# A log-sum-exp kernel on one core: VectorE's jump behind the last sum, checks joined, one exponential for four folded rows, the small logarithm one piece later

## The chip, the core and the metric

One core of a Trainium2 chip runs the kernel. The metric is device time in microseconds of one execution; a median of several runs is given, and one more execution is recorded by the hardware profiler. Shorter is better.

## The reference

The input is 32 x 512 rows of 1024 fp32 numbers, 64 MiB in all; the output is one number for each row.

```python
def reference(x):
    max_x = np.max(x, axis=-1, keepdims=True)
    return (max_x.squeeze(-1) + np.log(np.sum(np.exp(x - max_x), axis=-1))).astype(np.float32)
```

## The kernel before

The kernel takes the exponential without subtracting the maximum, adds up, and takes the logarithm. Beside that it checks that every sum lies between 1e-15 and 1e15 (and that the first elements of one row aren't too large); a flag is read back, and only where a check fails a slow path inside an `If` computes everything anew with the maximum. On ordinary data that path is skipped.

The 16384 rows are 128 partitions times 128 rows. The first 112 rows of each partition (`W`) come in nine loads (`LOADS`) into a ring of 48 rows in the on-chip memory; all loads are issued by SyncE (SP), each as soon as the users of the buffer that it overwrites are done. The string beside each size in `LOADS` says how the load is summed. Each word is one exponential on ScalarE (ACT), in place:

- `R16`: VectorE (DVE) sums 16 whole rows with one reduction (L237).
- `F4`: GpSimd (POOL) first adds the second half of each of four rows to the first (L231), and VectorE later sums the half rows (L190, `reduce_folded`). A pending fold is summed at the next `F`, or after the next `R`.

The last 16 rows of each partition (`B`) come in nine late pieces (`late`), cut at sizes of their own and not at rows: 3760 elements from the first rows, 3488 from the last four, then 2656, 2000, 1456, 1088 and 800 through the middle, then the last row's end (610 with two joining numbers) and the first row's head (530 with two). Each gets one exponential (L280, the last two L273 and L265). After each, VectorE sums the rows that have become complete, one instruction for a row, which adds the row's halves and accumulates (L199, `halves`); the profile shows a second, short instruction for each, the read of the accumulator. The first and last rows are each split over two pieces. The part of each that comes early is summed by itself (`parts`), and the logarithm of half of it is written twice into the ring beside the piece that comes late (`joined`, the small logarithm of L310, on 4 numbers), so that the exponential of that piece, which accumulates, adds it in.

When the second late piece is through, ScalarE takes the logarithms of the first 112 rows (L302), and VectorE checks these sums and the two parts (`check_early`, L159 and L164). The sums of the late rows are added up on TensorE (PE) in `count` (L177, `add_up`), so that a number that isn't finite shows there.

At the end ScalarE takes the logarithms of 15 late rows (L321) and of the first late row (L323), SyncE stores them (L325), VectorE checks the 15 sums (L330) and the head's elements (L340), PE adds the outcome to `count`, and VectorE turns it into the flag `fine` (L347). ScalarE and VectorE read it and branch over the slow path (L403). SyncE waits for that and for the stores, and resets the semaphores (L406, L408).

Waits are written by hand: `Counted.wait` lets an engine wait for another's count, and instructions of one engine run in program order. The line `nc.vector.addr_align(128, offset=0, max_nops=0)` (L284) puts the next VectorE instruction at a multiple of 128 instruction slots; the padding is jumped over. In the kernel before it stands ahead of the sum of the row that the 800-wide piece completes, which is VectorE's last row sum.

Of the kernel before, what the change touches and what calls it, by code (L numbers as in the profile page):

```python
# [12 lines left out]
LOW, HIGH = 1e-15, 1e15  # L13
# [3 lines left out]
B = 16  # L17
# [4 lines left out]

LOADS = [
    (16, "R16"), (16, "R16"), (16, "R16"), (16, "F9 R7"), (13.5, "F6 R7"), (12.5, "R7 F6"),
    (9, "R5 F4"), (7, "F4 R3"), (6, "F2 F2 R2"),
]


# [28 lines left out]
def kernel(  # L57
# [5 lines left out]
    nc = tc.nc  # L63
# [4 lines left out]
    P = nc.NUM_PARTITIONS  # L68
    fp32 = mybir.dt.float32
    i32 = mybir.dt.int32  # L70
    AF = mybir.ActivationFunctionType
    AX = mybir.AxisListType
    ALU = mybir.AluOpType

    x_flat = x.flatten_outer_dims()
    n, d = x_flat.shape
    assert n % P == 0
    NC = n // P
    H = d // 2
    W = NC - B  # L80
# [6 lines left out]
    def source(e0, size):  # L87
# [1 line left out]
        return x_rest[:, e0 - W * d : e0 - W * d + size] if e0 >= W * d else x_rows[:, e0 : e0 + size]  # L89

    loads = [
        (int(size * d), [(op[0], 0 if op[0] == "Y" else int(op[1:] or 1)) for op in ops.split()])
        for size, ops in LOADS
    ]
    assert sum(size for size, _ in loads) == W * d
    assert sum(s for _, ops in loads for _, s in ops) == W
    start = MID * d - sum(PIECES)
    late = [(HEAD, start), (MID * d, B * d - BACK)]
    for size in PIECES:
# [1 line left out]
        start += size  # L101
    late += [(B * d - BACK, B * d), (0, HEAD)]
    assert start == MID * d and sum(e - s for s, e in late) == B * d

    def sbuf(name, cols, dtype=fp32, rows=P):
        return nc.alloc_sbuf_tensor(name, [rows, cols], dtype).ap()

    ring = sbuf("ring", RING * d)
    sums_all = sbuf("sumexp", 2 + NC)
    parts, sumexp = sums_all[:, 0:2], sums_all[:, 2 : 2 + NC]  # L110
    res = sbuf("res", NC)
    clamped = sbuf("clamped", NC)
    bad = sbuf("bad", 3)
# [11 lines left out]
    act = Counted(nc, nc.scalar, "act")  # L125
    dve = Counted(nc, nc.vector, "dve")
    pe = Counted(nc, nc.tensor, "pe")
    pool = Counted(nc, nc.gpsimd, "pool")
# [25 lines left out]
        ]  # L154

    def check_early():
        n = 2 + W
        dve.wait(dve, dve.n)
        dve.did(nc.vector.tensor_scalar(  # L159
            out=clamped[:, 0:n], in0=sums_all[:, 0:n],  # L160
            scalar1=LOW, scalar2=HIGH, op0=ALU.max, op1=ALU.min,
        ))
        dve.wait(dve, dve.n)
        dve.did(nc.vector.scalar_tensor_tensor(  # L164
            out=clamped[:, 0:n], in0=clamped[:, 0:n], scalar=0.0, in1=sums_all[:, 0:n],
            op0=ALU.bypass, op1=ALU.not_equal, accum_out=bad[:, 0:1],
        ))
        pe.wait(dve, dve.n)
        pe.did(nc.tensor.matmul(count, lhsT=bad[:, 0:1], rhs=far, start=True, stop=False))  # L169
# [3 lines left out]
    def add_up():  # L173
        while sums:
            c, who, at = sums.pop(0)
            pe.wait(who, at)
            pe.did(nc.tensor.matmul(  # L177
                count, lhsT=ones, rhs=sumexp[:, c : c + 1], start=False, stop=False
            ))

    folded = []
# [15 lines left out]
    def halves(v, c):  # L197
        n = v.shape[1] // 2
        return dve.did(nc.vector.scalar_tensor_tensor(  # L199
            out=v[:, 0:n], in0=v[:, 0:n], scalar=1.0, in1=v[:, n : 2 * n],  # L200
            op0=ALU.mult, op1=ALU.add, accum_out=c,
        ))

    c = 0
    p = 0
# [4 lines left out]
    for i, (size, ops) in enumerate(loads):  # L210
        if here + size > RING * d:
            assert here == p
            p = here = 0
        if any(q < here + size and q + t * d > here for _, t, q, _ in folded):
            reduce_folded()
        dma = load(i, here, done_before, size)
        if i < AHEAD:
            first_loads.extend(x.ins for x in dma)
        end = here + size
        done_before += size  # L220
        act.wait(landed[i], 16 * len(dma))
        for k, (how, s) in enumerate(ops):
            rows = ring[:, p : p + s * d].rearrange("p (c d) -> p c d", d=d)
            upto = end if k + 1 == len(ops) else p + s * d
            v = ring[:, here:upto]
            at = act.did(nc.scalar.activation(out=v, in_=v, func=AF.Exp))  # L226
            here = upto
            if how == "F":
                reduce_folded()
                pool.wait(act, at)  # L230
                at = pool.did(nc.gpsimd.tensor_tensor(  # L231
                    out=rows[:, :, 0:H], in0=rows[:, :, 0:H], in1=rows[:, :, H:d], op=ALU.add
                ))
                folded.append((c, s, p, at))
            else:
                dve.wait(act, at)
                at = dve.did(nc.vector.reduce_sum(out=sumexp[:, c : c + s], in_=rows, axis=AX.X))  # L237
                users.append((p, p + s * d, dve, at))
                early_sum = at
                reduce_folded()  # L240
            c += s
            p += s * d
        assert here == end
# [4 lines left out]
    def place(e0):  # L248
        return e0 - MID * d + p if e0 >= MID * d else gap + GAP + e0

    joins = bass.AP(
        tensor=ring.tensor, offset=ring[:, gap : gap + 1].offset,
        ap=[ring.ap[0], [GAP - 2, 2], [1, 2]],
    )
    summed = set()
    seen = []
    for k, (s, e) in enumerate(late):
        i = len(loads) + k
        at0, at1 = place(s), place(s) + e - s
        [dma] = load(i, at0, W * d + s, e - s)  # L260
        act.wait(landed[i], 16)
        if k >= len(late) - 2:
            act.wait(act, joined)
        if k == len(late) - 1:
            head_sum = act.did(nc.scalar.activation(  # L265
                out=last_exp[:, 0 : e - s + 2], in_=ring[:, at0 - 2 : at1], func=AF.Exp,
                accum_out=last_sum,
            ))
            break
        if k == len(late) - 2:  # L270
            assert at1 == gap
            v = ring[:, at0 : at1 + 2]
            back_sum = act.did(nc.scalar.activation(  # L273
                out=v, in_=v, func=AF.Exp, accum_out=sumexp[:, NC - 1 : NC]
            ))
            sums.append((NC - 1, act, back_sum))
            add_up()
            continue
        v = ring[:, at0:at1]
        at = act.did(nc.scalar.activation(out=v, in_=v, func=AF.Exp))  # L280
        if k == 0:
            reduce_folded()
        if k == len(late) - 3:
            nc.vector.addr_align(128, offset=0, max_nops=0)  # L284
        dve.wait(act, at)
        seen.append((s, e))
        for r in range(1, B - 1):
            left = r * d
            for s0, e0 in sorted(seen):
                if s0 <= left < e0:  # L290
                    left = e0
            if r not in summed and left >= (r + 1) * d:
                summed.add(r)
                row = ring[:, place(r * d) : place(r * d) + d]
                sums.append((W + r, dve, halves(row, sumexp[:, W + r : W + r + 1])))
        if k == 0:
            halves(ring[:, at0 : place(0) + d], parts[:, 1:2])
        if k == 1:
            halves(ring[:, place((B - 1) * d) : at1], parts[:, 0:1])
            both = dve.n  # L300
            act.wait(dve, early_sum)
            ln_early = act.did(nc.scalar.activation(  # L302
                out=res[:, 0:W], in_=sumexp[:, 0:W], func=AF.Ln
            ))
            check_early()
        if k >= 1:
            add_up()
        if k == 2:
            act.wait(dve, both)
            joined = act.did(nc.scalar.activation(  # L310
                out=joins, in_=parts[:, :, None].to_broadcast([P, 2, 2]), func=AF.Ln, scale=0.5
            ))
    assert len(summed) == B - 2

# [1 line left out]
    sp.wait(landed[-2], 16)  # L316
    nc.sync.dma_start(out=out_rows, in_=res[:, 0:W]).then_inc(sp.sem, 16)

    act.wait(dve, dve.n)
    act.wait(act, back_sum)  # L320
    act.did(nc.scalar.activation(out=res[:, W + 1 : NC], in_=sumexp[:, W + 1 : NC], func=AF.Ln))  # L321
    act.wait(act, head_sum)
    act.did(nc.scalar.activation(out=res[:, W : W + 1], in_=last_sum, func=AF.Ln))  # L323
    sp.wait(act, act.n)
    nc.sync.dma_start(out=out_rest, in_=res[:, W:NC]).then_inc(stored, 16)  # L325


    dve.wait(dve, dve.n)
    dve.wait(act, back_sum)
    dve.did(nc.vector.scalar_tensor_tensor(  # L330
        out=clamped[:, W + 1 : NC], in0=sumexp[:, W + 1 : NC], scalar=LOW,
        in1=sumexp[:, W + 1 : NC], op0=ALU.max, op1=ALU.not_equal, accum_out=bad[:, 1:2],
    ))
    pe.wait(dve, dve.n)
    pe.did(nc.tensor.matmul(count, lhsT=bad[:, 1:2], rhs=far, start=False, stop=False))
    pe.wait(dve, less_at)
# [4 lines left out]
        out=over, in0=ring[:, at0 : at0 + half], scalar=CEILING,  # L341
        in1=ring[:, at0 + half : at1], op0=ALU.max, op1=ALU.max, accum_out=bad[:, 2:3],
    ))
    pe.wait(dve, dve.n)
    at = pe.did(nc.tensor.matmul(count, lhsT=bad[:, 2:3], rhs=steep, start=False, stop=True))  # L345
# [12 lines left out]
    with nc.If(all_fine < 1):  # L358
# [3 lines left out]
        rows = 0  # L362
# [100 lines left out]
```

## Time and profile before

| | us |
|---|---|
| median of 3 runs | 161.93 (161.88 to 162.07) |
| profiled execution, its own time | 161.83 |
| its span, first to last instruction | 160.1 |
| ScalarE busy | 114.5 |
| VectorE busy | 114.2 |
| GpSimd busy | 37.3 |
| PE busy | 2.5 |

The DMA queue that loads the input moves 67.18 MB in all and has packets under way for 97.8% of 16 engines' span. Times in the profile are counted from the span's start; 1.7 of the profiled execution's own time lie outside the span. The first 116 us are the same kind of work in larger portions. The change touches what comes after the ninth load has landed, at about 138, so the views shown below are of that end.

### The profile page before, as it was taken

Reading aid. Unit: us, or ns where it says so; the run is one execution under the profiler, and the core shown is the slowest. Engines: PE = TensorE matmul, PEld = TensorE weight load, DVE = VectorE, ACT = ScalarE, POOL = GpSimd, SP = SyncE. Lnnn points to the kernel's source line nnn. Section 1 sums busy time; section 2 is a strip of 40 time slices with the busy share of each in tenths; the row PEclk is TensorE's granted clock in tenths of the full one; section 3 lists DMA queues with packets and bytes.
Section 4 is the critical chain, followed back from the end, with each engine's and each line's share of the span. In section 5 each row is a group of like instructions: output and inputs, shape, how many; then the busy total and the mean of one; then the engine's idle time right before and its main releaser. Section 6 shows DMA issues by size and latency. Waiting matters only on the chain.

```text
span 160.1 us, 250 instructions
## 1 busy us (share of the span) xinstructions
PE 2.5 (2%) x38; PEld 1.3 (1%) x38; DVE 114.2 (71%) x60; ACT 114.5 (71%) x32; POOL 37.3 (23%) x11
## 2 busy tenths in 40 slices
PE   0000000000000000000000000000000000000033
PEld 0000000000000000000000000000000000000011
DVE  0000000019999499994999859959999999999986
ACT  3000059980799709995099949992999989799996
POOL 0000000000000000000000993690004979891000
DMA  8995996996996996997999999999999999999993
GB/s 319 507 507 254 507 524 262 524 524 262 524 524 262 524 524 262 524 475 311 483 442 442 442 426 409 409 409 472 405 396 454 458 409 393 421 437 425 414 402 114
DMA packets 3025, 67.18 MB, mean 420 GB/s; under 512 B 592, under 2 KB 592, under 8 KB 1488
## 3 DMA queue, kind: packets, MB, share of 16 engines
q1 hardware_dynamic: 3024, 67.18, 97.8%
q14 instruction: 1, 0.01, 0.0%
HBM read 67.11 MB, written 0.07 MB: 419 GB/s over the span
## 4 chain that ended last, share of the span: by engine, by line
DMA 51%; ACT 27%; DVE 20%; issue 0%; PE 0%
DMA ring<-in_x_dram 51%; ACT ring L226 19%; DVE sumexp L237 16%; ACT ring L280 7%; DVE sumexp L190 2%; DVE ring L199 2%; DVE over L340 0%; PE count L345 0%; ACT res L302 0%; DVE clamped L330 0%; DVE fine L347 0%; ACT ring L310 0%
## 5 line engine op out<-in xcount | busy, mean ns | idle before, releaser
L226 ACT ACTIVATE ring<-ring 128x16384 f32<-128x16384 f32 (+9 forms) x16 | 98.0, 6169 | 42.3 <-DMA ring<-in_x_dram 42.3
L237 DVE TENSOR_REDUCE sumexp<-ring 128x16 f32<-128x16384 f32 (+4 forms) x9 | 85.6, 9514 | 42.0 <-ACT ring L226 42.0
L231 POOL TENSOR_TENSOR ring<-ring 128x3072 f32<-128x3072 f32 (+3 forms) x7 | 37.1, 5314 | 107.1 <-ACT ring L226 107.1
L190 DVE TENSOR_REDUCE sumexp<-ring 128x6 f32<-128x3072 f32 (+3 forms) x7 | 18.4, 2659 | 0.0
L280 ACT ACTIVATE ring<-ring 128x3760 f32<-128x3760 f32 (+6 forms) x7 | 13.7, 2006 | 0.0
L199 DVE SCALAR_TENSOR_TENSOR ring<-ring 128x512 f32<-128x512 f32 (+2 forms) x16 | 9.6, 652 | 0.4 <-ACT ring L280 0.3
L135 ACT ACT_TABLE_LOAD x1 | 1.3, 1283 | 1.9 <-PEq L66 1.9
L169 PE MATMUL count<-far,bad 128*1 128x1 f32 x2 | 0.2, 164 | 152.6 <-DVE clamped L164 152.6
L177 PE MATMUL count<-sumexp,ones 128*1 128x1 f32 x30 | 2.0, 163 | 3.6 <-DVE ring L199 3.5
L136 DVE MEMSET ones<- 128x1 f32 x1 | 0.1, 59 | 2.0 <-PEq L66 2.0
L169 PEld LDWEIGHTS count<-far,bad 128*1 128x1 f32 x2 | 0.1, 82 | 152.6 <-DVE clamped L164 152.6
L199 DVE DVE_READ_ACCUMULATOR ring<-ring 128x1 f32 x16 | 1.4, 85 | 0.0
L177 PEld LDWEIGHTS count<-sumexp,ones 128*1 128x1 f32 x30 | 1.1, 81 | 4.5 <-DVE ring L199 4.5
L273 ACT ACTIVATE ring<-ring 128x610 f32<-128x610 f32 x1 | 0.7, 696 | 0.0
L265 ACT ACTIVATE last_exp<-ring 128x530 f32<-128x530 f32 x1 | 0.6, 595 | 0.0
L340 DVE SCALAR_TENSOR_TENSOR over<-ring 128x264 f32<-128x264 f32 x1 | 0.4, 428 | 0.0
L347 DVE TENSOR_SCALAR fine<-count 1x1 int32<-1x1 f32 x1 | 0.1, 146 | 0.3 <-PE count L345 0.3
L164 DVE SCALAR_TENSOR_TENSOR clamped<-clamped,sumexp 128x114 f32<-128x114 f32 x1 | 0.3, 279 | 0.0
L302 ACT ACTIVATE res<-sumexp 128x112 f32<-128x112 f32 x1 | 0.3, 278 | 0.0
L159 DVE TENSOR_SCALAR clamped<-sumexp 128x114 f32<-128x114 f32 x1 | 0.2, 221 | 0.0
L321 ACT ACTIVATE res<-sumexp 128x15 f32<-128x15 f32 x1 | 0.2, 203 | 0.0
L330 DVE SCALAR_TENSOR_TENSOR clamped<-sumexp 128x15 f32<-128x15 f32 x1 | 0.2, 174 | 0.0
(20 smaller groups left out, 2.3 us busy)
## 6 DMA issues: line engine op xcount, KB each, us to landing
ring<-in_x_dram SPq DMA_DIRECT2D x1, 7936.0 KB, 21.2
ring<-in_x_dram SPq DMA_DIRECT2D x1, 6912.0 KB, 23.9
ring<-in_x_dram SPq DMA_DIRECT2D x1, 6400.0 KB, 19.7
ring<-in_x_dram SPq DMA_DIRECT2D x1, 4608.0 KB, 15.9
ring<-in_x_dram SPq DMA_DIRECT2D x1, 3584.0 KB, 24.0
ring<-in_x_dram SPq DMA_DIRECT2D x1, 3072.0 KB, 19.1
ring<-in_x_dram SPq DMA_DIRECT2D x1, 1880.0 KB, 16.0
ring<-in_x_dram SPq DMA_DIRECT2D x1, 1744.0 KB, 19.8
```

What stands on the lines that cost most here:

```text
L135: nc.scalar.preload_act_table_set("natural_log_exp_and_others")
L169: pe.did(nc.tensor.matmul(count, lhsT=bad[:, 0:1], rhs=far, start=True, stop=False))
L177: pe.did(nc.tensor.matmul(count, lhsT=ones, rhs=sumexp[:, c : c + 1], start=False, stop=False))
L190: at = dve.did(nc.vector.reduce_sum(out=sumexp[:, c0 : c0 + s0], in_=halves, axis=AX.X))
L199: return dve.did(nc.vector.scalar_tensor_tensor(out=v[:, 0:n], in0=v[:, 0:n], scalar=1.0, in1=v[:, n : 2 * n], op0=ALU.mult, op1=ALU.add, ...
L226: at = act.did(nc.scalar.activation(out=v, in_=v, func=AF.Exp))
L231: at = pool.did(nc.gpsimd.tensor_tensor(out=rows[:, :, 0:H], in0=rows[:, :, 0:H], in1=rows[:, :, H:d], op=ALU.add))
L237: at = dve.did(nc.vector.reduce_sum(out=sumexp[:, c : c + s], in_=rows, axis=AX.X))
L265: head_sum = act.did(nc.scalar.activation(out=last_exp[:, 0 : e - s + 2], in_=ring[:, at0 - 2 : at1], func=AF.Exp, accum_out=last_sum,))
L273: back_sum = act.did(nc.scalar.activation(out=v, in_=v, func=AF.Exp, accum_out=sumexp[:, NC - 1 : NC]))
L280: at = act.did(nc.scalar.activation(out=v, in_=v, func=AF.Exp))
L340: dve.did(nc.vector.scalar_tensor_tensor(out=over, in0=ring[:, at0 : at0 + half], scalar=CEILING, in1=ring[:, at0 + half : at1], op0=ALU.m ...
```

## The change

Four edits:

- The ninth load, `F2 F2 R2`, becomes `F2+2 R2`: one exponential over four rows in place of two over two rows each. GpSimd still folds them as two pairs, and VectorE still sums two pairs. Since both folds are pending when the two straight rows come, VectorE sums the straight rows first and both pairs after them; before, the first pair came ahead of the straight rows.
- The jump moves from ahead of VectorE's last row sum to behind it, ahead of the final check.
- The checks are joined: the first row's early part now lies in that row's column of the sums, so that one early check covers the first 112 rows, both parts and the three late rows summed with the first late piece. The final check covers 12 sums instead of 15, and the three rows are no longer added up on PE. The final check is written ahead of the last logarithms, and ScalarE's wait ahead of the logarithms of the 15 rows is now for this check instead of the last row sum.
- The small logarithm (`joined`) is taken after the exponential of the 2000-wide piece instead of the 2656-wide one.

```diff
-    (9, "R5 F4"), (7, "F4 R3"), (6, "F2 F2 R2"),
+    (9, "R5 F4"), (7, "F4 R3"), (6, "F2+2 R2"),
...
+    LATE = W + late[0][1] // d
...
-    sums_all = sbuf("sumexp", 2 + NC)
-    parts, sumexp = sums_all[:, 0:2], sums_all[:, 2 : 2 + NC]
+    sums_all = sbuf("sumexp", 1 + NC)
+    sumexp = sums_all[:, 1 : 1 + NC]
+    part_15, part_0 = sums_all[:, 0:1], sumexp[:, W : W + 1]
...
     def check_early():
-        n = 2 + W
+        n = 1 + LATE
...
             c, who, at = sums.pop(0)
+            if c < LATE:
+                continue
...
-                at = pool.did(nc.gpsimd.tensor_tensor(
-                    out=rows[:, :, 0:H], in0=rows[:, :, 0:H], in1=rows[:, :, H:d], op=ALU.add
-                ))
-                folded.append((c, s, p, at))
+                r = 0
+                for m in groups:
+                    lo = rows[:, r : r + m, 0:H]
+                    at = pool.did(nc.gpsimd.tensor_tensor(
+                        out=lo, in0=lo, in1=rows[:, r : r + m, H:d], op=ALU.add
+                    ))
+                    folded.append((c + r, m, p + r * d, at))
+                    r += m
...
-        if k == len(late) - 3:
-            nc.vector.addr_align(128, offset=0, max_nops=0)
         dve.wait(act, at)
...
-        if k == 2:
+        if k == 3:
             act.wait(dve, both)
             joined = act.did(nc.scalar.activation(
-                out=joins, in_=parts[:, :, None].to_broadcast([P, 2, 2]), func=AF.Ln, scale=0.5
+                out=joins, in_=parts, func=AF.Ln, scale=0.5
             ))
...
+    nc.vector.addr_align(128, offset=0, max_nops=0)
+    dve.wait(dve, dve.n)
+    dve.wait(act, back_sum)
+    dve.did(nc.vector.scalar_tensor_tensor(
+        out=clamped[:, LATE:NC], in0=sumexp[:, LATE:NC], scalar=LOW,
+        in1=sumexp[:, LATE:NC], op0=ALU.max, op1=ALU.not_equal, accum_out=bad[:, 1:2],
+    ))
     act.wait(dve, dve.n)
-    act.wait(act, back_sum)
     act.did(nc.scalar.activation(out=res[:, W + 1 : NC], in_=sumexp[:, W + 1 : NC], func=AF.Ln))
     act.wait(act, head_sum)
     act.did(nc.scalar.activation(out=res[:, W : W + 1], in_=last_sum, func=AF.Ln))
     sp.wait(act, act.n)
     nc.sync.dma_start(out=out_rest, in_=res[:, W:NC]).then_inc(stored, 16)
-
-
-    dve.wait(dve, dve.n)
-    dve.wait(act, back_sum)
-    dve.did(nc.vector.scalar_tensor_tensor(
-        out=clamped[:, W + 1 : NC], in0=sumexp[:, W + 1 : NC], scalar=LOW,
-        in1=sumexp[:, W + 1 : NC], op0=ALU.max, op1=ALU.not_equal, accum_out=bad[:, 1:2],
-    ))
```

More of the change, by code (lines that the diff above doesn't have):

```diff
@@ L91 @@
     loads = [
-        (int(size * d), [(op[0], 0 if op[0] == "Y" else int(op[1:] or 1)) for op in ops.split()])
+        (int(size * d), [(op[0], [int(s) for s in op[1:].split("+")]) for op in ops.split()])
         for size, ops in LOADS
@@ L95 @@
     assert sum(size for size, _ in loads) == W * d
-    assert sum(s for _, ops in loads for _, s in ops) == W
+    assert sum(sum(s) for _, ops in loads for _, s in ops) == W
     start = MID * d - sum(PIECES)
@@ L108 @@
     ring = sbuf("ring", RING * d)
-    sums_all = sbuf("sumexp", 2 + NC)
-    parts, sumexp = sums_all[:, 0:2], sums_all[:, 2 : 2 + NC]
+    sums_all = sbuf("sumexp", 1 + NC)
+    sumexp = sums_all[:, 1 : 1 + NC]
+    part_15, part_0 = sums_all[:, 0:1], sumexp[:, W : W + 1]
+    parts = bass.AP(
+        tensor=sums_all.tensor, offset=sums_all.offset,
+        ap=[sums_all.ap[0], [1 + W, 2], [0, 2]],
+    )
     res = sbuf("res", NC)
@@ L221 @@
         act.wait(landed[i], 16 * len(dma))
-        for k, (how, s) in enumerate(ops):
+        for k, (how, groups) in enumerate(ops):
+            s = sum(groups)
             rows = ring[:, p : p + s * d].rearrange("p (c d) -> p c d", d=d)
@@ L296 @@
         if k == 0:
-            halves(ring[:, at0 : place(0) + d], parts[:, 1:2])
+            halves(ring[:, at0 : place(0) + d], part_0)
         if k == 1:
-            halves(ring[:, place((B - 1) * d) : at1], parts[:, 0:1])
+            halves(ring[:, place((B - 1) * d) : at1], part_15)
             both = dve.n
```

## The prediction

> **What bounds the kernel now.** I read the chain of waits first, then the stages of the end, then the landings of single loads against the starts of the exponentials that consume them. The chain (start, length, what):
>
> ```profile
> 137.97 5.51 ACT ring L226 x3
> ...
> 155.44 1.10 DVE ring L199 x3
> ```
>
> From here the end looks like ScalarE's (ACT): from 137.97 the chain runs over the exponentials of the ninth load and then over those of the late pieces, and VectorE (DVE) comes in at 155.44. An edit that shortens ScalarE should then pay in full. The stages (busy time by engine, then granted clock, DMA share, GB/s) give a second candidate:
>
> ```profile
> core 0: us, PE busy (x) PEld busy (x) DVE busy (x) ACT busy (x) POOL busy (x), PEclk, DMA share, GB/s
> 137.90:143.40 5.50, 0.00 (x0) 0.00 (x0) 5.50 (x3) 5.43 (x4) 4.79 (x3) 1.00 1.01 432
> 149.60:154.00 4.40, 0.87 (x18) 0.56 (x18) 4.03 (x17) 4.40 (x6) 0.00 (x0) 1.00 1.00 411
> ```
>
> DMA, ScalarE and VectorE are all full, so no busy share decides. What decides is which of them is later at each piece. For three of the late pieces I take the issue (time, length) and the time to landing from the DMA view of the same instant, and then the exponentials:
>
> ```profile
> 127.70 0.46 SPq L150 DMA_DIRECT2D ring<-in_x_dram  x1
> ring<-in_x_dram SPq DMA_DIRECT2D x1, 1000.0 KB, 24.4
> 135.44 0.33 SPq L150 DMA_DIRECT2D ring<-in_x_dram  x1
> ring<-in_x_dram SPq DMA_DIRECT2D x1, 728.0 KB, 18.5
> 136.81 0.44 SPq L150 DMA_DIRECT2D ring<-in_x_dram  x1
> ring<-in_x_dram SPq DMA_DIRECT2D x1, 304.0 KB, 20.3
> ```
>
> ```profile
> 152.20 1.85 ACT L280 ACTIVATE ring<-ring 128x2000 f32<-128x2000 f32 x1
> 153.99 1.42 ACT L280 ACTIVATE ring<-ring 128x1456 f32<-128x1456 f32 x1
> 155.34 1.11 ACT L280 ACTIVATE ring<-ring 128x1088 f32<-128x1088 f32 x1
> 156.35 0.85 ACT L280 ACTIVATE ring<-ring 128x800 f32<-128x800 f32 x1
> 157.11 0.70 ACT L273 ACTIVATE ring<-ring 128x610 f32<-128x610 f32 x1
> ```
>
> Issue plus landing: 152.10, 153.94 and 157.11, each good to 0.05. The exponentials of these pieces (2000, 1456 and 610 wide) start at 152.20, 153.99 and 157.11. ScalarE shows no idle time, yet each start lies within 0.1 of its landing. Transfer and ScalarE are level all along the end: an exponential that is ready earlier finds its data missing. Being earlier on ScalarE alone is worth a few hundredths of a microsecond at most; being later counts, once it exceeds the same few hundredths.
>
> The finish, after the head's exponential and its read of the accumulator:
>
> ```profile
> 158.34 0.12 ACT L265 ACTIVATION_READ_ACCUMULATOR last_exp<-ring 128x1 f32 x1
> 158.39 0.20 ACT L321 ACTIVATE res<-sumexp 128x15 f32<-128x15 f32 x1
> 158.69 0.34 SPq L325 DMA_DIRECT2D out_dram<-res  x1
> out_dram<-res SPq DMA_DIRECT2D x1, 8.0 KB, 1.4
> SPq L408 <- SPq L408: 0.4, 1, 0.4
> ```
>
> The last store goes at 158.69 and lands 1.4 later, at 160.1, which is the span's end. The last row is the DMA issuer's (SyncE's) wait: it idles 0.4 before its final instruction, so the verdict on the checks, which the chain of waits ends with, has some 0.4 to spare, and the logarithms and the store set the end.
>
> **The change, edit by edit.**
>
> *One exponential for four rows.* Means by shape, and the engines around it:
>
> ```profile
> L226 ACT ACTIVATE ring<-ring 128x4096 f32<-128x4096 f32 x2 | 7.2, 3608 | 0.5 <-DMA ring<-in_x_dram 0.5
> L226 ACT ACTIVATE ring<-ring 128x2048 f32<-128x2048 f32 x3 | 5.5, 1898 | 1.0 <-DMA ring<-in_x_dram 1.0
> 139.95 4.68 POOL L231 TENSOR_TENSOR ring<-ring 128x1024 f32<-128x1024 f32 x2 [0.71 <-ACT ring L226]
> 140.78 2.28 DVE L190 TENSOR_REDUCE sumexp<-ring 128x4 f32<-128x2048 f32 x1
> 144.10 2.28 DVE L237 TENSOR_REDUCE sumexp<-ring 128x2 f32<-128x2048 f32 x1
> 146.29 1.21 DVE L190 TENSOR_REDUCE sumexp<-ring 128x2 f32<-128x1024 f32 x1
> 147.42 0.69 DVE L199 SCALAR_TENSOR_TENSOR ring<-ring 128x512 f32<-128x512 f32 x1
> ```
>
> Busy time falls by 2 x 1.898 - 3.608 = 0.19. But neighbours overlap: three of 1.898 would be 5.69, and the three together take 5.51, so each joint hides 0.09. One joint goes, and ScalarE gains 0.19 - 0.09 = 0.10.
>
> GpSimd (POOL) pays: its first fold waits for all four rows, until 137.97 + 3.61 + 0.08 = 141.66 instead of 139.95 (0.08 as now between an exponential's end and the fold). The two folds take 2.34 each and end near 144.0 and 146.3.
>
> VectorE's order changes with it. Now: the eighth load's four folded rows (140.78 to 143.06), the first folded pair, the two straight rows at 144.10, the second pair at 146.29, the first late row at 147.42. After: the straight rows come second and have to wait for their exponential, which starts 0.10 earlier than now and ends at 137.97 + 5.51 - 0.10 = 143.38; so they start at 143.41. They take 2.19 to the next start (144.10 to 146.29), so the first pair comes at 145.60, and with 1.13 each (146.29 to 147.42) the second at 146.73, 0.4 after its fold has ended, and the first late row at 147.86. VectorE is 0.44 late, for it stands idle from 143.06 to 143.41 and hides less of its overlap. What hides this 0.44:
>
> ```profile
> 153.06 0.69 DVE L199 SCALAR_TENSOR_TENSOR ring<-ring 128x512 f32<-128x512 f32 x1
> ...
> 154.08 0.69 DVE L199 SCALAR_TENSOR_TENSOR ring<-ring 128x512 f32<-128x512 f32 x1 [0.33 <-ACT ring L280]
> 154.70 0.69 DVE L199 SCALAR_TENSOR_TENSOR ring<-ring 128x512 f32<-128x512 f32 x1
> ```
>
> The sum at 153.06 would start at 153.50 and leave VectorE free 0.62 later (154.08 to 154.70), at 154.12, where the next sum starts at 154.08 now. The idle time there takes in all but 0.04, and the sum at 155.44, bound by its exponential, takes in that rest (154.12 + 2 x 0.62 = 155.36). Without this cover the price would be up to 0.44.
>
> *Small logarithm one piece later.* It occupies ScalarE for the 0.10 between 152.10 and 152.20:
>
> ```profile
> 152.10 0.19 ACT L310 ACTIVATE ring<-sumexp 128x4 f32<-128x4 f32 x1
> ```
>
> The 2000-wide exponential may start up to 0.10 earlier, but its piece lands at 152.10 (up to 152.15), so it starts near 152.16. It occupies ScalarE for 1.76 (1.85 less the 0.09 of overlap), to 153.92; then the logarithm, 0.10; then the 1456-wide one at 154.02 instead of 153.99. That one occupies 1.33, to 155.35, against 155.34 now. So 0.03 late at one exponential and 0.00 to 0.01 at the next. It waits for VectorE's second edge part, which is done before 152.10 now and so before 152.54 then: late for the old place, in time for the new one. Queued behind it on ScalarE is the 1456-wide exponential, already counted. Nothing at the end.
>
> *The jump and the final check.* VectorE at the end, the jump, and the one instruction packet:
>
> ```profile
> 157.28 0.69 DVE L199 SCALAR_TENSOR_TENSOR ring<-ring 128x512 f32<-128x512 f32 x1
> 157.90 0.08 DVE L199 DVE_READ_ACCUMULATOR ring<-ring 128x1 f32 x1
> 158.01 0.17 DVE L330 SCALAR_TENSOR_TENSOR clamped<-sumexp 128x15 f32<-128x15 f32 x1
> 158.12 0.08 DVE L330 DVE_READ_ACCUMULATOR clamped<-sumexp 128x1 f32 x1
> L284 DVEq COMPARE_BRANCH  x1: 51/51/51, 156.5 to 156.5; - x1
> q14 instruction: 1, 0.01, 32.9%
> ```
>
> The jump runs at 156.5, as soon as the sum before it has been released by the exponential that ends at 156.45. Behind it the last sum starts at 157.28, just when its forerunner ends: the jump costs nothing visible, and less than 0.8 in any case. At its new place it runs when the last sum is released, after the exponential that ends at 157.20, so at 157.25. What follows, the check, waits anyway for the last row's sum (157.90 + 0.08 = 157.98): with the jump's 0.05, a cover of 0.68 again. Bounds: nothing, as now, or the whole fetch of rival B; I take 0, by the row of the same jump 0.8 earlier.
>
> [...]
>
> The final check keeps its place, 0.03 late at most by the exponential at 154.02: done at 158.23. The new wait is ScalarE's: the 15 logarithms now need this check, not just the last sum. Queued behind that wait are the last logarithm and then the store, the end itself. It costs nothing as long as the check is done before 158.36, because ScalarE is busy with the accumulator until 158.39. The reserve is about 0.13; each further delay of VectorE goes one to one into the end.
>
> *The smaller edits*: three more columns in the early check, three fewer in the final one, three fewer sums in the count on PE, one ScalarE wait fewer. None lies on a path that sets the end; 0. DMA: the late loads wait for buffers of earlier loads than the ninth, and the last but one is issued at 136.81 with the last right behind it, before the ninth load's first exponential at 137.97, so their times stay.
>
> **Sum**: -0.10 on ScalarE caught by the landings, +0.44 on VectorE caught by its idle time, +0.03 on the way, 0 at the store. The span stays 160.1 and the profiled execution 161.83; the median of the runs is 161.93, 0.10 above, and is the forecast. Bounds: -0.10 if landings don't hold ScalarE, +0.31 if the 0.44 reaches the check unabsorbed (0.44 - 0.13).
>
> **Rivals.**
>
> *A, ScalarE is the bound* in most executions and its 0.10 reaches the store: 161.83. For it: the chain names ScalarE. Against it: the three landings. It counts within 0.2% of the median (0.32), which is about what a measurement of this kernel can tell from no change.
>
> *B, slower: the jump is exposed.* If the jump makes VectorE fetch the code that it goes to, VectorE stops at its last step. The instruction packet is in the window from 157.6 to 157.7, its slice begins at 157.66, and it took 0.329 x 16 x 0.1 = 0.53: 1.69 from the jump at 156.5 to the packet's end. After the change that would be 157.25 + 1.69 = 158.94, the check would be done near 159.15, the logarithms 0.79 late, and the time 162.72. It decides from a stall of about 0.8, where the cover of 0.68 and the reserve of 0.13 are used up. Against it: the last sum ran at 157.28, before that packet had begun, so the code behind the jump was there already and the packet is for something later.
>
> *C, slower: VectorE's 0.44 is not absorbed*, for instance because the folds run longer beside other work than the 2.34 here: up to +0.31, 162.24, still at the edge of no change. For it: VectorE has almost no idle time left after 147.86.
>
> *D, nothing of the schedule shifts*, because the joined exponential overlaps no better than the pair did: VectorE's order changes all the same; 161.93.
>
> **Chances.** Forecast with D 0.59, A 0.15, C 0.12 (a third of it over the bound, where the folds run longer still), B 0.05; 0.09 for what I do not see, two thirds of it fast, such as transfers that end earlier with the late fetch. Together: within 0.2% 0.59 + 0.15 + 0.08 = 0.82, slower 0.04 + 0.05 + 0.03 = 0.12, faster by over 0.2% 0.06. Range 161.75 to 162.25: A below, C above, and the spread of the runs; B and the unseen lie outside.
>
> **What would show it.** Right: one 4096-wide exponential at 137.97 of 3.6, the next at about 143.3; straight rows summed at 143.4 and the first late row near 147.86; no idle VectorE before the sum at 154.1; the 1088-wide exponential still at 155.34; the jump near 157.25 and the check at 158.0 to 158.05; the 15 logarithms at 158.39; the store at 158.69. Wrong: a gap between the last sum and the check (B); idle ScalarE ahead of the logarithms, released by the check (C or B); the head's exponential clearly earlier than 157.8 with the landings earlier too.

## The result, and the profile after

| | before | after |
|---|---|---|
| median of 10 runs each, us | 161.97 (161.85 to 162.08) | 161.55 (161.45 to 161.62) |
| ratio of the changed kernel to before | | 0.9974, 95% interval 0.9966 to 0.9982 |
| profiled execution, its own time | 161.83 | 161.53 |
| its span | 160.14 | 160.20 |
| its time outside the span | 1.69 | 1.33 |

The kernel became 0.26% faster, 0.42 us, where no change was forecast; 161.55 lies below the range. But the recorded span did not become shorter: it is 0.06 longer. All of the gain lies in the 1.7 us that the prediction set aside as lying outside the span.

Inside the span the forecast held. ScalarE, in order of time (start, length, operation):

```profile
138.01 5.42 ACT L236 ACTIVATE ring<-ring 128x4096 f32<-128x4096 f32 x2 [1.03 <-DMA ring<-in_x_dram]
143.33 6.41 ACT L294 ACTIVATE ring<-ring 128x3760 f32<-128x3760 f32 x2
...
152.24 1.87 ACT L294 ACTIVATE ring<-ring 128x2000 f32<-128x2000 f32 x1
154.01 0.19 ACT L322 ACTIVATE ring<-sumexp 128x4 f32<-128x4 f32 x1
154.11 3.17 ACT L294 ACTIVATE ring<-ring 128x1456 f32<-128x1456 f32 x3
157.19 0.70 ACT L287 ACTIVATE ring<-ring 128x610 f32<-128x610 f32 x1
...
158.42 0.12 ACT L279 ACTIVATION_READ_ACCUMULATOR last_exp<-ring 128x1 f32 x1
158.47 0.20 ACT L339 ACTIVATE res<-sumexp 128x15 f32<-128x15 f32 x1
```

The two exponentials of the ninth load take 5.42 in place of the three's 5.51: 0.09 shorter, as worked out. That is gone by the 2000-wide exponential, which starts at 152.24 (before 152.20), 0.02 behind the landing of its piece at 152.21; everything from here runs 0.04 to 0.12 behind before, and the ninth load itself had landed 0.04 later. VectorE:

```profile
143.46 2.29 DVE L251 TENSOR_REDUCE sumexp<-ring 128x2 f32<-128x2048 f32 x1 [0.37 <-ACT ring L236]
145.66 2.34 DVE L199 TENSOR_REDUCE sumexp<-ring 128x2 f32<-128x1024 f32 x2
147.92 0.68 DVE L208 SCALAR_TENSOR_TENSOR ring<-ring 128x512 f32<-128x512 f32 x1
...
154.14 0.69 DVE L208 SCALAR_TENSOR_TENSOR ring<-ring 128x512 f32<-128x512 f32 x1
...
157.38 0.69 DVE L208 SCALAR_TENSOR_TENSOR ring<-ring 128x512 f32<-128x512 f32 x1
157.99 0.08 DVE L208 DVE_READ_ACCUMULATOR ring<-ring 128x1 f32 x1
158.11 0.17 DVE L334 SCALAR_TENSOR_TENSOR clamped<-sumexp 128x12 f32<-128x12 f32 x1
158.21 0.08 DVE L334 DVE_READ_ACCUMULATOR clamped<-sumexp 128x1 f32 x1
```

It waits 0.37 for the straight rows and comes to the first late row 0.50 later than before; by the sum at 154.14 (154.08 before) only 0.06 is left. The jump, by the view of its line:

```profile
L331 DVEq COMPARE_BRANCH  x1: 51/51/51, 157.3 to 157.3; - x1
```

The last store in the timeline, its landing in the list of DMA issues (KB, us to landing), and the issuer's last wait:

```profile
158.76 0.34 SPq L343 DMA_DIRECT2D out_dram<-res  x1
```

```profile
out_dram<-res SPq DMA_DIRECT2D x1, 8.0 KB, 1.4
```

```profile
SPq L419 <- SPq L419: 0.3, 1, 0.3
```

The jump is where it was expected, hidden under the last sum. The check is read out at 158.21 + 0.08 = 158.29, ahead of the logarithms at 158.47, which follow directly on ScalarE's own work, and the store lands at 160.2.

### The profile page after: what moved, and what is told of

It reads as the page before. It is cut to its first block, busy times and chain, and to the rows that moved or that the text cites. A ratio compares the mean times of both kernels' runs of the same rounds, so it can differ in the third digit from the quotient of the medians.

```text
span 160.2 us, 236 instructions
## 1 busy us (share of the span) xinstructions
PE 2.3 (1%) x32; PEld 1.2 (1%) x32; DVE 114.2 (71%) x60; ACT 114.5 (71%) x31; POOL 37.3 (23%) x11
## 4 chain that ended last, share of the span: by engine, by line
DMA 51%; ACT 27%; DVE 20%; issue 0%; PE 0%
DMA ring<-in_x_dram 51%; ACT ring L236 19%; DVE sumexp L251 16%; ACT ring L294 7%; DVE sumexp L199 2%; DVE ring L208 2%; DVE over L351 0%; PE count L356 0%; ACT res L314 0%; DVE clamped L334 0%; DVE fine L358 0%; ACT ring L322 0%
```

## The experiments

The measure used here is the time outside the span: each run's time less its span (listed to 0.1), averaged over the runs of a kernel. It is a difference of two lengths and does not say at which end of the span the time lies. The mean span is the average of the same runs' spans. The time outside is 1.70 for the kernel before, in 12 to 33 runs beside each experiment (1.69 to 1.71), and 1.35 for the changed one.

### Is it the jump?

e1 moves the jump alone; e2 takes the changed kernel and puts the jump back; e3 and e4 leave the jump out of the kernel before and of the changed one.

```diff
 # e1, from before; e2 is the reverse, from after
-        if k == len(late) - 3:
-            nc.vector.addr_align(128, offset=0, max_nops=0)
...
+    nc.vector.addr_align(128, offset=0, max_nops=0)
     dve.wait(dve, dve.n)
     dve.wait(act, back_sum)
```

> The kernel before with the jump moved behind the last row sum, ahead of the final check, and nothing else. The changed kernel has a span 0.06 longer than before (160.20 against 160.14) and is 0.42 faster, so the gain lies outside the span: 1.69 there before, 1.33 after. Theory J (the place of the jump, by when it runs or by what code lies behind it, sets the time outside the span): 161.6, span 160.1, 1.3 to 1.4 outside. Theory N (the number of instructions and waits on the other engines sets it: 12 PE rows, one exponential and one wait fewer): as before, 161.97, 1.7 outside. Theory S (the shifted schedule of VectorE and ScalarE at the end): as before.

> The changed kernel with the jump back ahead of the last row sum, all else as changed. J: 162.0, 1.7 outside the span. N and S: as after, 161.55, 1.33 outside.

> The kernel before with the jump left out. J, if what counts is that code behind the jump is aligned and fetched early: slower than before, by some tenths, outside the span. J, if the jump itself costs and later is merely cheaper: faster than before, 161.5 or less. N, S: as before, 161.97.

> The changed kernel with the jump left out. J, by alignment: slower than after, and as e3. J, by the jump's own cost: no slower than after. N, S: as after, 161.55.

| | median | ratio to before | outside the span | mean span |
|---|---|---|---|---|
| e1 | 161.94 | 1.0001 (0.9992 to 1.0010) | 1.71 | 160.26 |
| e2 | 161.58 | 0.9977 (0.9968 to 0.9986) | 1.33 | 160.26 |
| e3 | 162.36 | 1.0025 (1.0016 to 1.0034) | 1.69 | 160.67 |
| e4 | 161.99 | 1.0004 (0.9995 to 1.0013) | 1.36 | 160.64 |
| before | 161.93 | | 1.70 | 160.24 |

Theory J falls: the place of the jump changes nothing, and the rest of the change carries the whole gain. Having a jump matters, but inside the span: the mean is 160.67 and 160.64 without it, 160.24 before. VectorE in e3:

```profile
157.96 0.08 DVE L199 DVE_READ_ACCUMULATOR ring<-ring 128x1 f32 x1
158.08 0.17 DVE L328 SCALAR_TENSOR_TENSOR clamped<-sumexp 128x15 f32<-128x15 f32 x1
158.54 0.08 DVE L328 DVE_READ_ACCUMULATOR clamped<-sumexp 128x1 f32 x1 [0.28 <-issue]
158.56 0.43 DVE L338 SCALAR_TENSOR_TENSOR over<-ring 128x264 f32<-128x264 f32 x1
```

The check's read starts 0.46 after the check, where with the jump it is 0.11 (158.01 and 158.12 before), and nothing that the profile shows is waited for ("issue"). Without the jump VectorE stalls 0.35 there (0.31 in e4); with it, in either place, no stall shows at the check (0.11 before, 0.10 after). That it is then hidden under the long row sums is argued, not shown.

The mean span grows by 0.43 in e3 and 0.4 in e4, but not through this stall alone. In e3 the logarithms do not wait for the check. The last store in e3's timeline, and its landing in the list of DMA issues:

```profile
158.76 0.34 SPq L323 DMA_DIRECT2D out_dram<-res  x1
```

```profile
out_dram<-res SPq DMA_DIRECT2D x1, 8.0 KB, 1.8
```

The store is issued 0.07 later than before and takes 1.8 to land in place of 1.4 (1.6 in e4); it lands at 160.56, where the profiled span ends (160.57). The one packet of the instruction queue runs behind the store's issue, from 159.19 for 0.42; before it runs at 157.66. That it holds up the landing would fit, but is not shown.

### Which of the other edits?

e5 has only the schedule (one exponential for four rows, and the later small logarithm); e6 only the joined checks, with the final check ahead of the logarithms and the three sums fewer on PE that belong to them; e7 only the three sums fewer on PE; e8 only the final check ahead of the logarithms, with ScalarE's own wait gone.

```diff
 # e7, from before
             c, who, at = sums.pop(0)
+            if W < c < W + 4:
+                continue
...
 # e8, from before: the three statements of the final check stand here now
+    dve.wait(dve, dve.n)
+    dve.wait(act, back_sum)
+    dve.did(nc.vector.scalar_tensor_tensor(
...
     act.wait(dve, dve.n)
-    act.wait(act, back_sum)
```

> The kernel before with one exponential for the four folded rows and the small logarithm one piece later; jump and checks as before. The runs so far: without the jump's move the changed kernel keeps its gain (0.36 outside the span), and the move alone gives nothing, so J fell. Theory S (the schedule, or ScalarE's stream being one exponential shorter): 161.6, 1.3 outside the span. Theory C (the joined checks: PE's shorter stream, or ScalarE's wait): 161.95, 1.7 outside.

> The kernel before with the joined checks, the final check ahead of the logarithms, and three sums fewer on PE; ninth load, small logarithm and jump as before. S: 161.95, 1.7 outside the span. C: 161.6, 1.3 outside.

> The kernel before without the three late rows' sums on PE (12 PE rows fewer); their check for numbers that aren't finite is left out. Theory P (PE's stream, three matmuls shorter, ends outside the span): 161.6, 1.3 outside. Otherwise 161.95, 1.7 outside.

> The kernel before with the final check written ahead of the last logarithms, which then wait for it, and without ScalarE's wait of its own for the back piece's sum; all else as before. Theory W (ScalarE's stream, one wait shorter, ends outside the span): 161.6, 1.3 outside. Otherwise 161.95, 1.7 outside.

| | median | ratio to before | outside the span | ScalarE's instructions, from before |
|---|---|---|---|---|
| e5 | 161.83 | 0.9994 (0.9985 to 1.0004) | 1.50 | -1 (an exponential) |
| e6 | 161.77 | 0.9992 (0.9983 to 1.0002) | 1.53 | -1 (a wait) |
| e7 | 161.93 | 0.9997 (0.9987 to 1.0007) | 1.69 | 0 |
| e8 | 161.74 | 0.9989 (0.9979 to 0.9999) | 1.51 | -1 (a wait) |
| before | 161.90 | | 1.70 | |

S, C and W had each foreseen the whole gain or none; instead two quite different edits save half each (0.20 in e5, 0.19 in e8). The ratios hardly tell them from before, but the time outside the span does: its single values lie between 1.44 and 1.63 in e5, e6 and e8, and between 1.64 and 1.76 for before. What the two edits have in common is one instruction fewer on ScalarE. PE's rows don't matter (e7: 1.69).

### The length of ScalarE's stream

e9 and e12 add two idle exponentials (of one column, their output not used) at the start of ScalarE's stream, where it waits 18.5 us for data, to the changed kernel and to before; e10 and e11 give ScalarE a jump of its own ahead of the ninth load.

```diff
 # e9, e12
+    tiny = sbuf("tiny", 2)
+    act.wait(dve, 1)
+    for q in range(2):
+        nc.scalar.activation(out=tiny[:, q : q + 1], in_=ones, func=AF.Exp)
...
 # e10, e11
+        if i == len(loads) - 1:
+            nc.scalar.addr_align(128, offset=0, max_nops=0)
         act.wait(landed[i], 16 * len(dma))
```

> The changed kernel with two exponentials of one column each added on ScalarE at the very start, where it idles for 21 us (their output is not used). So far, mean time outside the span: before 1.70; one exponential fewer (e5) 1.50; one wait fewer (e8) 1.51; both (after) 1.35; PE's rows or the jump change nothing. Theory L (the length of ScalarE's instruction stream, wherever the instructions stand, decides by 0.18 each): 1.70 outside, 161.9. Theory E (what counts is ScalarE's work at the end: fewer joints and waits there let it finish sooner): 1.35 outside, 161.55.

> The kernel before with the same two idle exponentials at the start. L, if each instruction goes on costing: 2.05 outside, 162.3. L, if the stream's end meets a border of a fetch block and the cost has a ceiling: 1.7 or less, 161.95 or less. E: 1.70, 161.95.

> The kernel before with a jump like VectorE's on ScalarE too, ahead of the ninth load's exponentials, where ScalarE idles 1.04: the code behind it starts at a multiple of 128 slots. Theory B (a border between blocks of instructions lies in what ScalarE runs after the span, and an instruction more or less shifts it): the border is gone from there, 1.35 outside or less, 161.6 or less. L without a border: 1.7 or more. E: 1.70.

> The changed kernel with the same jump on ScalarE. B: the same time outside the span as e10, since both have the same code in the same places behind the jump but for two instructions; 161.55 or less. L without a border: 1.4 or more, 161.6. E: 1.35.

| | median | ratio to before | outside the span | mean span |
|---|---|---|---|---|
| e9 | 161.97 | 1.0004 (0.9995 to 1.0014) | 1.72 | 160.30 |
| e12 | 161.60 | 0.9982 (0.9973 to 0.9992) | 1.32 | 160.30 |
| e10 | 161.87 | 0.9996 (0.9986 to 1.0005) | 1.34 | 160.57 |
| e11 | 162.00 | 1.0006 (0.9996 to 1.0015) | 1.35 | 160.64 |
| before | 161.93 | | 1.70 | 160.24 |

Two idle instructions, 135 us ahead of the stage that was changed (3.2 and 138), undo the whole gain of the changed kernel (e9: 1.72). Theory E falls. The same two make the kernel before as fast as the changed one (e12: 1.32): more instructions, less time, so "each instruction costs" falls too. And with the code behind a jump on ScalarE aligned to 128 slots, both kernels have the same 1.34 to 1.35 (e10, e11). That is what theory B foresaw. It supposes a border between blocks of instructions near the end of ScalarE's stream; no view shows the border itself.

The jump on ScalarE costs its gain elsewhere. In e10, ScalarE's jump by the view of its line, the instruction queue (q14) in the DMA view of the 0.1 us from 134.6 (packets, MB, share of 16 engines), and ScalarE's timeline at the ninth load:

```profile
L222 ACTq COMPARE_BRANCH  x1: 33/33/33, 130.8 to 130.8; - x1
```

```profile
q14 instruction: 1, 0.01, 19.3%
```

```profile
138.55 1.91 ACT L228 ACTIVATE ring<-ring 128x2048 f32<-128x2048 f32 x1 [1.47 <-DMA ring<-in_x_dram]
```

A packet of this queue runs among the loads, for 0.193 x 16 x 0.1 = 0.31; the ninth load's exponential starts at 138.55 and not at 137.97, and the mean span is 0.33 longer than before's. The packet starts some 3.8 behind the jump here, and not the 1.2 that e15's expectation takes over from VectorE's jump (156.5 and 157.66 before).

### Is it a border, and where does it lie?

e13 adds one idle exponential at the start and e16 adds 128; e15 (from before) and e14 (from after) put ScalarE's jump ahead of the head's exponential, when the loads are over; e17 adds two instructions in the slow path, which isn't run.

```diff
 # e13: as e12 with 1 in place of 2; e16: with 128
...
 # e15, e14
+        if k == len(late) - 1:
+            nc.scalar.addr_align(128, offset=0, max_nops=0)
         act.wait(landed[i], 16)
...
 # e17, inside nc.If(all_fine < 1)
+        for q in range(2):
+            nc.scalar.activation(out=tiny[:, q : q + 1], in_=sumexp[:, q : q + 1], func=AF.Ln)
         nc.scalar.activation(out=res, in_=sumexp[:, 0:NC], func=AF.Ln).then_inc(ready, 1)
```

> The kernel before with one idle exponential at the start of ScalarE's stream. Mean time outside the span by the length of that stream, counted from before: -2: 1.34; -1: 1.51; 0: 1.70; +2: 1.32. Theory B (a border of a block): between, 1.32 to 1.70. Theory R (no border, an odd or even count or chance): 1.51 as for -1, or 1.70.

> The kernel before with 128 idle exponentials of one column at the start of ScalarE's stream, in its idle time before the first landing at 21.7. B with blocks of 128: the same place relative to the border as before, so 1.70 outside the span, about 161.95; one more packet of instructions early. R: 1.32 to 1.5, as for other added instructions.

> The kernel before with the jump on ScalarE late: ahead of the head's exponential, when all loads have been read. B: 1.34 outside the span, and no cost in the span, since the packet that follows 1.2 after a jump comes after the loads and not among them as in e10 (span 160.6); so 161.55 to 161.6, the whole gain of the change from one line. If the jump is exposed on ScalarE: span up by 0.3.

> The changed kernel with the same late jump on ScalarE. B: as after, 161.55 (its end is already clear of the border, 1.34 outside). Faster than after only if after still pays a part of the border.

> The kernel before with two logarithms of one column added on ScalarE inside the slow path, which the branch skips. So far, mean time outside the span by instructions added to ScalarE's stream: -2: 1.34; -1: 1.51; 0: 1.70; +1: 1.52; +2: 1.32; +128: 1.67. Theory A (the border lies behind the slow path, in what ScalarE runs after the span): the code behind it shifts by two, 1.33 outside, 161.6. Theory F (it lies ahead of the branch): nothing shifts there, 1.70, 161.95.

| | median | ratio to before | outside the span | mean span |
|---|---|---|---|---|
| e13 | 161.74 | 0.9988 (0.9979 to 0.9998) | 1.52 | 160.26 |
| e16 | 162.33 | 1.0024 (1.0015 to 1.0034) | 1.67 | 160.62 |
| e15 | 161.62 | 0.9979 (0.9969 to 0.9989) | 1.34 | 160.35 |
| e14 | 161.59 | 0.9980 (0.9971 to 0.9990) | 1.35 | 160.27 |
| e17 | 161.52 | 0.9972 (0.9962 to 0.9982) | 1.34 | 160.22 |
| before | 161.90 (e17: 161.97) | | 1.70 (e17: 1.69) | 160.23 (e17: 160.33) |

Ordered by what is added to ScalarE's stream, the time outside the span is 1.34 (-2), 1.51 (-1), 1.70 (0), 1.52 (+1), 1.32 (+2), 1.67 (+128): a peak of 0.36 just on the kernel before, gone two instructions away on either side, and there again 128 instructions on. These counts alone do not fix the length of a block at 128, since a shorter length that divides 128 would bring the peak back there too. Four falls: behind their jump e10 and e11 end two instructions apart, and both have 1.34 to 1.35. Eight or more is not excluded. For 128 speaks the instruction queue in the DMA view of the whole span (packets, MB, share), before and in e16:

```profile
q14 instruction: 1, 0.01, 0.0%
q14 instruction: 2, 0.02, 0.0%
```

So with 128 instructions more there is one packet more, of 0.01 MB; that a packet is one block is argued, not shown. (It comes at 11.6, among the first loads, and e16's mean span is 0.39 longer, much as with the packet in e10.)

e17 gives the whole gain of the change (1.34 outside), with nothing different in any instruction that runs inside the span: by theory B, what the border delays lies behind the slow path in ScalarE's code, so it is what ScalarE runs last. e15 gives the gain outside the span (1.34) by one line on ScalarE. e14 shows that nothing is left to gain there by this means: 1.35 like after itself. No kernel of the study beats the changed one clearly: e17 is as fast.

The cause is settled this far: the gain depends on where the end of ScalarE's code falls among the instruction slots, and instructions that do no work move it either way (e9 1.72, e12 1.32, e17 1.34). So the gain was luck. The kernel before happened to lie on the worst place of those tried; one instruction more on ScalarE would have gained half of it as well (e13: 1.52), two all of it (e12: 1.32).

The views show no record from behind the span, but the packed traces also hold the times of semaphore updates, and these go on there. In the profiled executions the last of them stands 1.46 behind the span's end in before (1.69 outside) and e9 (1.70) as in the changed kernel, e12 and e17 (1.33 to 1.34), so none of the 0.36 arises ahead of that update. In e13 alone, of all runs, the update before the last comes at 1.53 and not at 1.41 to 1.44. That fits a border which the added instructions move across ScalarE's very last steps; which engine made the late update isn't shown. Not shown either is what ScalarE runs there, why the time outside is longer by 0.18 with one instruction on either side (e8, e13) and by 0.36 at its worst (before), and whether 1.33 is a floor that something else sets, another engine perhaps.

## Why the prediction was wrong, point by point

- **Landings hold ScalarE**: right. The 0.10 saved there measured 0.09 and was gone at the 2000-wide exponential.
- **VectorE late by 0.44, taken in by its idle time**: right in kind; 0.50 (the ninth load landed 0.04 later, and the straight rows started at 143.46 and not at 143.41; the two pairs took the 2.26 that was reckoned), of which 0.06 was left at 154.14.
- **The small logarithm later, 0.03**: right in kind, 0.08 after the ninth load's 0.04 is allowed for (154.11 against 153.99).
- **The jump at no cost, the check's wait at no cost**: right; e1 confirms the first (1.0001). Rivals B and C did not happen. Rival A did not either: the head's exponential did not come earlier (157.88, before 157.81). Nor did D: the joint saved 0.09.
- **The step that failed** is the sum: "The span stays 160.1 and the profiled execution 161.83". It carried the 1.7 outside the span over as a constant. The term that it lacked is -0.36, from two edits that it put down to 0 at the end: the exponential saved, costed only by ScalarE's time in the span, and "one ScalarE wait fewer", listed under the smaller edits. Each takes an instruction from ScalarE's stream, and by theory B each moves what ScalarE runs last by one slot off a border: -0.20 (e5) and -0.19 (e8), together -0.35 to -0.37 (after, e2). The prediction gave 0.06 to a kernel faster by over 0.2%, but for causes inside the span.
- **The place of code was looked at on VectorE alone.** The prediction saw the one instruction packet behind VectorE's jump (157.66 and 156.5) and asked only whether that jump stalls; it did not ask where ScalarE's code ends. That place made 0.36 of the time outside the span: 1.70 before, 1.34 with two instructions more ahead of that end (e17), and 1.67 with 128 more (e16).

## What to carry to other kernels

Compare the time outside the span before and after a change, not the span alone: here 0.36 with the span unchanged came from nothing more than two instructions fewer on one engine, and 0.38 from two more (e12). Before such a gain is put down to an edit, add one or two idle instructions early, or in a path that is skipped, and see if the gain moves. Where it does, a jump to an aligned slot on that engine can take the luck out of it: here it left 1.34 to 1.35 outside the span in all four runs that have one on ScalarE (e10, e11, e14, e15). Where it stood mattered: ahead of the ninth load, with a packet of the instruction queue among the loads (e10), the mean span was 0.33 longer than before's, and ahead of the head's exponential 0.12 (e15) and 0.04 (e14).

## What the runs showed that was not expected

- At the end of ScalarE's code, up to 0.36 us of time outside the span by where that end falls: 1.70 before, 1.34 and 1.32 two instructions away on either side, 1.67 with 128 more. A border between blocks of 128 instructions fits these runs; no view shows it.
- On VectorE, inside the span and without the jump: 0.46 between two steps that otherwise follow in 0.11, listed as "issue". A border there too is argued, not shown, since no run shifts VectorE's code by an instruction or two. For it speaks that the one instruction packet comes 1.1 behind that check (158.08 and 159.19 in e3, 157.99 and 159.06 in e4) and with the jump 1.2 to 1.4 behind the jump (156.5 and 157.66 before, 157.2 and 158.64 in e1).
- A jump to an aligned slot took 33 ns on ScalarE (e10, e15) and 51 ns on VectorE (before, after, e1), and a packet of the instruction queue followed it, of 0.31 (e10) to 0.53 (before). On ScalarE the jump adds this packet (two in e10 and e15, one in before); on VectorE there is one without the jump as well (e3). With the packet among the loads the mean span is 0.33 longer in e10, where the packet lasts 0.31; in e11, with the jump in the same place, it is 0.44 longer than after's.
